# A convolution with residual: the last residual pair in one load, and a sign from VectorE ahead of the stores

## The chip, the core and the metric

The kernel runs on one core of a Trainium2 chip. The metric is the device time of one execution in microseconds; a kernel's time is the median over its executions. One execution was also recorded by the hardware profiler, and all durations and moments below are from that record, counted from the start of its span.

Five engines work side by side and meet only through semaphores: TensorE (PE) multiplies, VectorE (DVE) adds, ScalarE (ACT) converts and packs, GpSimd (POOL) clears small tiles, and SyncE (SP) issues transfers. The transfers of one issuing engine go into one queue, which 16 DMA engines share.

## What is computed

A 3 by 3 convolution with padding 1 over 16 images of 64 channels and 64 by 64 pixels, plus a residual of the output's shape, all in float32.

```python
batch, c_in, h, w, c_out, k = 16, 64, 64, 64, 64, 3
...
x_pad = np.pad(x, ((0, 0), (0, 0), (pad, pad), (pad, pad)), mode='constant')
...
output[b, co] += weight[co, ci, kh, kw] * x_pad[b, ci, kh:kh+h, kw:kw+w]
...
return (output + residual).astype(np.float32)
```

x, the residual and the output are 16.78 MB each, the weights 0.15 MB.

## The kernel before

Two images make a pair: 2 times 64 channels fill the 128 partitions, so a pair of x, of the residual or of the output is one block of 128 rows of 4096 pixels, 2 MB. There are eight pairs.

**Tiles.** `xr` holds three pairs of x as they are loaded. `xp` are four packed bf16 images: even rows of pixels in one half of the partitions, odd rows in the other. `wl` holds the rearranged weights. `ps` are two accumulators in PSUM, one image each. `ro` holds all eight pairs of the residual; the sums are written over it, and the output is stored from it.

**SyncE (lines 144 to 160 and 258 to 259)** sets the order of nearly all transfers. It loads the pairs of x, each from the fourth on when ScalarE has read the buffer it goes to (`s_half`, line 147). Behind some of them come loads of the residual, as the list `RES` says (lines 41 to 49): each entry is which pairs, which part of the pixels (`WHOLE`, `LEFT`, `RIGHT`), and the pair of x that it follows. The entry without such a number, pair 0, is issued by ScalarE at the very start. Entry i of `RES` counts on semaphore `s_r[i % 3]`, and its load waits until the entry three places before has landed (line 87). The last pair of the residual comes in two entries, 5 and 6: its left and its right half.

Then SyncE waits on line 157 until entry 5, the left half, has landed. After that it issues the early stores (`EARLY`, line 39): pairs 0 and 1, pairs 2 and 3, pairs 4 and 5, pair 6. Each waits in addition for VectorE's count of first adds, `s_add`, to show that its pairs are done, which is known from the first add of the image behind them (line 159). The last pair is stored in two halves after the block, when everything else is done (lines 258 and 259).

**ScalarE** packs each image by two copies (lines 190 and 194).

**TensorE** does for each image 24 matmuls into one accumulator (lines 238 to 255). It waits for the packed image (`s_pack`) and for an accumulator that VectorE has read (`s_bank`); the waits of lines 240 and 241 also take one off these counts. When an image is done it raises `s_conv`.

**VectorE** (lines 203 to 226) first rearranges part of the weights (line 206), then for each image adds the residual in two steps: the even rows (`par` 0), which wait for `s_conv`, and the odd rows (`par` 1). The first step raises `s_add`, the second `s_bank`. Ahead of each pair's first image it waits until the entries of `RES` that the pair needs have landed (lines 216 to 218, by the helper on line 91).

**The semaphore `s_id`** counts preparations: 12 (`NZERO`) by GpSimd's clears, one by TensorE's transposes of the weights, one each by ScalarE and VectorE when the weights are rearranged. Thus it stands at `NZERO + 3` from then on.

Of the kernel before, what the change touches and what calls it, by code (L numbers as in the profile page):

```python
# [15 lines left out]
def kernel(  # L16
# [7 lines left out]
    nc = tc.nc  # L24
# [13 lines left out]
    NZERO = 4 + 2 * NXP  # L38
    EARLY = (slice(0, 2), slice(2, 4), slice(4, 6), slice(6, 7))
    WHOLE, LEFT, RIGHT = slice(0, NPIX), slice(0, NPIX // 2), slice(NPIX // 2, NPIX)  # L40
    RES = (
        (slice(0, 1), WHOLE, None),
        (slice(1, 2), WHOLE, 1),
        (slice(2, 4), WHOLE, 3),
        (slice(4, 6), WHOLE, 5),
        (slice(6, 7), WHOLE, 7),
        (slice(7, 8), LEFT, 7),
        (slice(7, 8), RIGHT, 7),
    )
    NR = 3  # L50

    res_bc = residual.rearrange("(p b) c h w -> (b c) p (h w)", b=2)
# [18 lines left out]
    s_x = [sem(f"s_x{i}") for i in range(NXR)]  # L71
    s_r = [sem(f"s_r{i}") for i in range(NR)]
    s_out = sem("s_out")
    s_id = sem("s_id")
# [6 lines left out]
    def load_x(p):  # L81
        return nc.sync.dma_start(out=xr[p % NXR][:, :], in_=x_bc[128 * p : 128 * p + 128, :]).then_inc(s_x[p % NXR], 16)

    def load_ro(i, e):
        pairs, cols, _ = RES[i]
        if i >= NR:
            e.wait_ge(s_r[i % NR], 16 * (i // NR))
        return e.dma_start(out=ro[:, pairs, cols], in_=res_bc[:, pairs, cols]).then_inc(s_r[i % NR], 16)

    def wait_ro(e, i):  # L90
        e.wait_ge(s_r[i % NR], 16 * (i // NR + 1))

    def store(pairs, cols=slice(0, NPIX)):
        return nc.sync.dma_start(out=out_bc[:, pairs, cols], in_=ro[:, pairs, cols])
# [21 lines left out]
    def to_the_front(dma):  # L116

        def fixed(ap):  # L120
            t = ap.bass_ap.tensor.name
            return mybir.PhysicalAccessPattern(
                ap=ap.ap, offset=ap.bass_ap.offset, dtype=ap.dtype, memref=t, memsetref=t + "_set", bass_ap=ap.bass_ap
            )

        front = nc.main_func.blocks[0].instructions
        here = nc.cur_bb.bb.instructions
        ins = here.pop()
        assert ins.name == dma.ins.name
        at = next(i for i, e in enumerate(front) if e.engine == ins.engine)  # L130
        front.insert(at, copy.replace(ins, ins=[fixed(a) for a in ins.ins], outs=[fixed(a) for a in ins.outs]))
# [5 lines left out]
    def weight_block(h, half, d, par, kh):  # L137

        at = 64 * half + 32 * h
        return dict(out=wl[at : at + 32, d, :, par, :], in_=tp[0:32, kh, 0:384].rearrange("p (kw co h) -> p kw co h", kw=3, h=2)[:, :, :, h])  # L140

    with tc.tile_critical(no_gpsimd_drain=True):  # L142

        for p in range(NPAIR):
            if p >= NXR:

                nc.sync.wait_ge(s_half, 2 * (p - NXR) + 3)
            if p == 0:
                to_the_front(load_x(p))
                nc.sync.dma_start(out=wraw[:, :], in_=w_rows[:, :]).then_inc(s_w, 16)  # L150
            else:
                load_x(p)
            for i, (_, _, behind) in enumerate(RES):
                if behind == p:
                    load_ro(i, nc.sync)

        wait_ro(nc.sync, len(RES) - 2)
        for pairs in EARLY:
            nc.sync.wait_ge(s_add, 2 * pairs.stop + 1)
            store(pairs).then_inc(s_out, 16)  # L160


        nc.gpsimd.memset(ident[:, :], 0.0).then_inc(s_id, 1)  # L163
        nc.gpsimd.wait_ge(s_id, 1)
        nc.gpsimd.affine_select(  # L165
            out=ident[:, :],
            in_=ident[:, :],
            compare_op=mybir.AluOpType.not_equal,
            fill=1.0,
            base=0,  # L170
            pattern=[[-1, 128]],
            channel_multiplier=1,
        ).then_inc(s_id, 1)
        nc.gpsimd.wait_ge(s_id, 2)
        for t in xp:
            nc.gpsimd.memset(t[0:64, 0, :], 0.0).then_inc(s_id, 1)  # L176
            nc.gpsimd.memset(t[64:128, J, :], 0.0).then_inc(s_id, 1)  # L177
        nc.gpsimd.memset(wl[0:64, 0, :, 1, :], 0.0).then_inc(s_id, 1)  # L178
        nc.gpsimd.memset(wl[64:128, 1, :, 0, :], 0.0).then_inc(s_id, 1)  # L179


        to_the_front(load_ro(0, nc.scalar))
        for n in range(B):
            p, im = divmod(n, 2)
            hp = slice(64 * im, 64 * im + 64)
            x4 = xr[p % NXR].rearrange("q (j two w) -> q j two w", two=2, w=W)
            t = xp[n % NXP]
            if im == 0:
                nc.scalar.wait_ge(s_x[p % NXR], 16 * (p // NXR + 1))
            i = nc.scalar.copy(out=t[64:128, 0:J, :], in_=x4[hp, :, 0, :])  # L190
            i.then_inc(s_half, 1)
            if n >= NXP:
                i._wait_ge(s_conv, n - NXP + 1)
            nc.scalar.copy(out=t[0:64, 1 : J + 1, :], in_=x4[hp, :, 1, :]).then_inc(s_pack, 1)  # L194
            if n == 0:
                nc.scalar.wait_ge(s_id, NZERO + 1)
                for b in blocks[4:]:
                    for h in range(2):
                        i = nc.scalar.copy(**weight_block(h, *b))  # L199
                i.then_inc(s_id, 1)  # L200


        nc.vector.wait_ge(s_id, NZERO + 1)
        for k, b in enumerate(blocks[:4]):
            for h in range(2):
                i = nc.vector.tensor_copy(**weight_block(h, *b))  # L206
                if k == h == 0:
                    i.then_inc(s_bank, 2)
        i.then_inc(s_id, 1)
        for n in range(B):  # L210
            p, im = divmod(n, 2)
            hp = slice(64 * im, 64 * im + 64)
            o4 = ro[:, p, :].rearrange("q (j two w) -> q j two w", two=2, w=W)
            psj = ps[n % 2].rearrange("q c j w -> q (c j) w")
            if im == 0:
                for i, (pairs, cols, _) in enumerate(RES):
                    if pairs.start <= p < pairs.stop:
                        wait_ro(nc.vector, i)
            for par in range(2):
                i = nc.vector.tensor_tensor(  # L220
                    out=o4[hp, :, par, :], in0=psj[64 * par : 64 * par + 64, :, :], in1=o4[hp, :, par, :], op=ADD
                )
                if par == 0:
                    i._wait_ge(s_conv, n + 1)

                i.then_inc(s_add if par == 0 or n == B - 1 else s_bank, 1)


        nc.tensor.wait_ge(s_id, NZERO)
        nc.tensor.wait_ge(s_w, 16)  # L230
        wraw3 = wraw.rearrange("p (ci t) -> p ci t", t=9)
        for t in range(9):
            i = nc.tensor.transpose(  # L233
                out=tp[0:32, t // 3, 128 * (t % 3) : 128 * (t % 3) + 128], in_=wraw3[:, :, t], identity=ident[:, :]
            )
        i.then_inc(s_id, 1)
        nc.tensor.wait_ge(s_id, NZERO + 3)
        with nc.Fori(0, B // NXP, 1, engines=[PE]):
            for n in range(NXP):
                nc.tensor.wait_ge(s_bank, 1).then_inc(s_bank, -1)  # L240
                nc.tensor.wait_ge(s_pack, 1).then_inc(s_pack, -1)  # L241
                order = [(1, 0), (1, 1), (0, 0), (0, 1), (2, 0), (2, 1)]
                for i, (kw, d) in enumerate(order):
                    xlo, xhi = max(0, 1 - kw), min(W, W + 1 - kw)
                    for c in range(NCHUNK):
                        j0 = JC * c
                        m = matmul(
                            ps[n % 2][:, c, :, xlo:xhi],
                            wl[:, d, kw, :, :].rearrange("q r c -> q (r c)"),
                            xp[n][:, j0 + d : j0 + d + JC, xlo + kw - 1 : xhi + kw - 1],  # L250
                            i == 0,
                            i == len(order) - 1,
                            c == 0,
                        )
                m.then_inc(s_conv, 1)
# [37 lines left out]
```

## Time and profile before

| What | Value |
|---|---|
| median of 4 runs | 122.37 us (122.27 to 122.47) |
| the profiled execution | 122.39 us |
| its span | 120.6 us |
| mean granted TensorE clock | 0.944 |
| TensorE busy | 86.8 us (72%), 389 instructions |
| VectorE busy | 76.0 us (63%), 40 instructions |
| ScalarE busy | 63.1 us (52%), 37 instructions |
| moved by DMA | 50.48 MB, mean 419 GB/s |
| read from and written to HBM | 33.70 MB, 16.78 MB |

The span is the part of the execution that the trace covers from the first to the last of the program's own instructions; the 1.8 us between it and the execution's time lie around it. The page cuts the span into 40 slices and shows for each engine a digit, the tenths of the slice in which it was busy; the row DMA does the same for the mean of the 16 DMA engines, and the row below it gives the bytes moved per time. The chain that ended last is followed back from the last instruction of an engine; transfers that nobody on the core waits for do not stand in it. The time of a transfer is shown from its issue to its landing, that is, until its semaphore has its full count.

### The profile page before, as it was taken

What the parts mean: (1) busy time and instruction counts of PE and PEld (TensorE: products, weight loads), DVE (VectorE), ACT (ScalarE), POOL (GpSimd) and SP (SyncE); (2) the same over time, 40 slices, a digit from 0 to 9 for tenths busy, and PEclk for the clock granted to TensorE, in tenths of its full rate; (3) what the DMA queues carried; (4) which work ended last, traced back from release to release, by engine and by line L of the source; (5) the groups of instructions that cost most, each with busy time, mean ns of one, the idle gap of its engine ahead of it and who ended that gap; (6) DMA issues with size and microseconds to landing.
All of it is one profiled execution on the core that took longest, in us unless ns stands there. A gap on an engine that the chain in (4) does not pass through costs nothing.

```text
span 120.6 us, 734 instructions
## 1 busy us (share of the span) xinstructions
PE 86.8 (72%) x389; PEld 10.7 (9%) x105; DVE 76.0 (63%) x40; ACT 63.1 (52%) x37; POOL 2.4 (2%) x16
## 2 busy tenths in 40 slices
PE   0000609999999999999999999999999999100000
PEld 0000300100111111111010101010101010000000
DVE  0000180069889898798989889898898989770000
ACT  4001999999999585795956859586500000000000
POOL 5200000000000000000000000000000000000000
PEclk9999999999999999999999999999999999975555
DMA  7999999999999999999999999999999999999994
GB/s 239 408 435 429 429 435 435 435 435 413 429 435 435 435 429 424 435 435 429 424 435 429 435 435 410 432 440 435 435 429 435 429 424 429 429 435 435 413 421 177
DMA packets 3808, 50.48 MB, mean 419 GB/s; under 512 B 352, under 2 KB 480, under 8 KB 480
## 3 DMA queue, kind: packets, MB, share of 16 engines
q1 hardware_dynamic: 3664, 48.38, 94.2%
q10 hardware_dynamic: 144, 2.10, 4.1%
HBM read 33.70 MB, written 16.78 MB: 419 GB/s over the span
## 4 chain that ended last, share of the span: by engine, by line
PE 70%; DVEq 2%; DVE 2%; issue 0%
PE ps L101 53%; PE ps L100 17%; DVEq L142 2%; DVE ro L220 2%
## 5 line engine op out<-in xcount | busy, mean ns | idle before, releaser
L220 DVE TENSOR_TENSOR ro<-ps,ro 64x2048 f32<-64x2048 f32 x32 | 73.2, 2288 | 16.8 <-PE ps L101 16.3
L101 PE MATMUL ps<-xp,wl 128*128 128x504 bf16 (+1 forms) x288 | 79.3, 385 | 0.2
L190 ACT CAST xp<-xr 64x2048 bf16<-64x2048 f32 x16 | 30.3, 1896 | 21.5 <-DMA xr<-in_x_dram 11.1
L100 PE MATMUL ps<-xp,wl 128*128 128x504 bf16 (+1 forms) x92 | 35.6, 387 | 3.4 <-PEq L241 3.4
L194 ACT CAST xp<-xr 64x2048 bf16<-64x2048 f32 x16 | 30.4, 1897 | 0.4
L100 PEld LDWEIGHTS ps<-xp,wl 128*128 128x128 bf16 x96 | 9.5, 99 | 78.2 <-issue 78.2
L206 DVE CAST wl<-ps 32x192 bf16<-32x192 f32 x8 | 2.8, 348 | 14.9 <-PE ps L233 14.7
L233 PE MATMUL ps<-ident,wraw 128*32 128x128 f32 x9 | 2.1, 416 | 12.6 <-DMA wraw<-in_weight_dram 12.6
L233 PEld LDWEIGHTS ps<-ident,wraw 128*32 128x32 f32 x9 | 1.2, 140 | 13.0 <-issue 12.5
L190 ACT ACT_TABLE_LOAD x1 | 1.3, 1283 | 1.1 <-SPq L142 1.1
L199 ACT CAST wl<-ps 32x192 bf16<-32x192 f32 x4 | 1.2, 306 | 0.0
L177 POOL MEMSET xp<- 64x64 bf16 x4 | 0.6, 146 | 0.2
L176 POOL MEMSET xp<- 64x64 bf16 x4 | 0.6, 144 | 0.2
L165 POOL TENSOR_SCALAR_AFFINE_SELECT ident<-ident 128x128 f32<-128x128 f32 x1 | 0.3, 293 | 0.2 <-POOL ident L163 0.2
L179 POOL MEMSET wl<- 64x192 bf16 x1 | 0.3, 253 | 0.1
L178 POOL MEMSET wl<- 64x192 bf16 x1 | 0.3, 251 | 0.1
L163 POOL MEMSET ident<- 128x128 f32 x1 | 0.2, 205 | 0.7 <-SPq L142 0.7
L277 POOL MEMSET const-bfloat16-1.0<- 128x1 bf16 x1 | 0.1, 112 | 0.0
L277 POOL MEMSET const-uint8-127<- 128x1 uint8 x1 | 0.1, 112 | 0.0
L277 POOL MEMSET const-float32-1.0<- 128x1 f32 x1 | 0.1, 108 | 0.0
L277 POOL MEMSET const-float32-0.0<- 128x1 f32 x1 | 0.1, 103 | 0.2 <-issue 0.2
## 6 DMA issues: line engine op xcount, KB each, us to landing
xr<-in_x_dram SPq DMA_DIRECT2D x8, 2048.0 KB, 14.8
out_dram<-ro SPq DMA_DIRECT2D x3, 4096.0 KB, 20.0
ro<-in_residual_dram SPq DMA_DIRECT2D x2, 4096.0 KB, 21.1
ro<-in_residual_dram SPq DMA_DIRECT2D x2, 2048.0 KB, 18.6
ro<-in_residual_dram ACTq DMA_DIRECT2D x1, 2048.0 KB, 12.0
ro<-in_residual_dram SPq DMA_DIRECT2D x2, 1024.0 KB, 19.2
out_dram<-ro SPq DMA_DIRECT2D x1, 2048.0 KB, 14.5
out_dram<-ro SPq DMA_DIRECT2D x2, 1024.0 KB, 10.3
```

The costliest lines, as they stand in the source:

```text
L100: return e.matmul(out=out_, lhsT=lhsT, rhs=rhs, start=start, stop=stop, skip_group_check=True)
L101: return e.add_instruction(mybir.InstMatmult(name=nc.get_next_instruction_name(), engine=PE, ins=[e.lower_ap(rhs), e.lower_ap(lhsT)], outs ...
L142: with tc.tile_critical(no_gpsimd_drain=True):
L176: nc.gpsimd.memset(t[0:64, 0, :], 0.0).then_inc(s_id, 1)
L177: nc.gpsimd.memset(t[64:128, J, :], 0.0).then_inc(s_id, 1)
L190: i = nc.scalar.copy(out=t[64:128, 0:J, :], in_=x4[hp, :, 0, :])
L194: nc.scalar.copy(out=t[0:64, 1 : J + 1, :], in_=x4[hp, :, 1, :]).then_inc(s_pack, 1)
L199: i = nc.scalar.copy(**weight_block(h, *b))
L206: i = nc.vector.tensor_copy(**weight_block(h, *b))
L220: i = nc.vector.tensor_tensor(out=o4[hp, :, par, :], in0=psj[64 * par : 64 * par + 64, :, :], in1=o4[hp, :, par, :], op=ADD)
L233: i = nc.tensor.transpose(out=tp[0:32, t // 3, 128 * (t % 3) : 128 * (t % 3) + 128], in_=wraw3[:, :, t], identity=ident[:, :])
L277: nc = _bacc.Bacc("TRN2", target_bir_lowering=False, num_devices=1)
```

## The change

The two entries of the last residual pair become one, of the whole pair. The list then has six entries, and the whole load takes the place of the left half, with the same semaphore and the same wait ahead of it.

SyncE no longer waits for a landing before the early stores. It waits until `s_id` reaches `NZERO + 4`. This last count comes from VectorE: a separate increment that stands in its program behind the first add of image 10 (counted from 0, so the eleventh) and ahead of that image's second add. The waits on `s_add` ahead of each early store stay as they are, and so do the two half stores of the last pair. The wait of VectorE ahead of pair 7 covers one entry in place of two.

```diff
         (slice(6, 7), WHOLE, 7),
-        (slice(7, 8), LEFT, 7),
-        (slice(7, 8), RIGHT, 7),
+        (slice(7, 8), WHOLE, 7),
     )
+    MANY = 10
...
-        wait_ro(nc.sync, len(RES) - 2)
+        nc.sync.wait_ge(s_id, NZERO + 4)
         for pairs in EARLY:
             nc.sync.wait_ge(s_add, 2 * pairs.stop + 1)
             store(pairs).then_inc(s_out, 16)
...
                 i.then_inc(s_add if par == 0 or n == B - 1 else s_bank, 1)
+                if par == 0 and n == MANY:
+                    nc.vector.sem_inc(s_id, 1)
```

## The prediction

> **What bounds the kernel now.** I read the page's strips of busy time first, then the chain, then the waits of SyncE's queue.
>
> ```profile
> DMA  7999999999999999999999999999999999999994
> GB/s 239 408 435 429 429 435 435 435 435 413 429 435 435 435 429 424 435 435 429 424 435 429 435 435 410 432 440 435 435 429 435 429 424 429 429 435 435 413 421 177
> ...
> q1 hardware_dynamic: 3664, 48.38, 94.2%
> ...
> PE 70%; DVEq 2%; DVE 2%; issue 0%
> ```
>
> The DMA row is full from the second slice to the last but one. The chain's shares add up to 74%: it runs along TensorE from 18.0 us to 103.1 and along VectorE to 107.7, and leaves the rest to transfers. So the stream of transfers is the bound. Check: 0.69 MB move in the first 3 us (view below); the other 49.79 MB at the 431 GB/s that the stretch from 3 to 60 us shows take 115.5 us, which ends at 118.5. Measured: the last store is issued at 108.36 us and lands 11.3 us later, at 119.7; the span ends at 120.6 and the run at 122.39. Only bytes, or a hole in the stream, can move the end.
>
> ```profile
> SPq L94 <- DVE ro L220: 20.7, 2, 10.7
> SPq L94 <- DMA ro<-in_residual_dram: 16.7, 1, 16.7
> ...
> SPq L88 <- DMA ro<-in_residual_dram: 1.5, 1, 1.5
> ```
>
> These are waits of SyncE's queue (total, times, longest). The 16.7 us is the wait that the change replaces: line 157, for the left half of the last residual pair. The 1.5 us is the right half's load, held until an earlier load lands; it goes too, since the whole load takes the left half's place and its semaphore. The 20.7 us are stores waiting for VectorE, which stay.
>
> **When the stores enter the queue, and what is then left in it.**
>
> ```profile
> 58.68 2.75 SPq L88 DMA_DIRECT2D ro<-in_residual_dram  x3
> 78.17 31.40 SPq L94 DMA_DIRECT2D out_dram<-ro  x6
> ```
>
> This is SyncE's timeline: pair 6 and the two halves of pair 7 are issued from 58.68 to 61.4, the first store at 78.17. Asked one at a time, the left half issues at 59.15 and lands 19.0 us later (78.15); the right half issues at 61.10 and lands 19.5 us later (80.6). The first store therefore has 2.4 us of the right half before it. I put the end of the right half's data between 79.7 and 80.1: at the end of the span the DMA share is 0.34 from 118.6 to 119.2 us and 0.00 after, so the last store's data end at 118.8 on average and by 119.2, 0.5 to 0.9 us before its landing; 80.6 less that is 79.7 to 80.1.
>
> ```profile
> 75.00:78.00 3.00, 3.00 (x15) 0.37 (x4) 2.42 (x2) 1.63 (x2) 0.00 (x0) 1.00 1.00 421
> 78.00:81.00 3.00, 3.00 (x15) 0.29 (x3) 2.97 (x2) 2.93 (x2) 0.00 (x0) 1.00 1.05 448
> 81.00:84.00 3.00, 3.00 (x15) 0.39 (x4) 2.42 (x2) 1.68 (x1) 0.00 (x0) 1.00 0.99 426
> ```
>
> The last two columns of these stretches are the DMA share and GB/s. Loads give way to stores at full share: there is no hole here that an earlier issue could close, so moving the stores forward gains nothing.
>
> **How late a store may be issued** follows from the start, where the queue is empty.
>
> ```profile
> DMA  0000000000000999907595700099559955909999
> ...
> DMA packets 42, 0.69 MB, mean 229 GB/s; under 512 B 0, under 2 KB 0, under 8 KB 0
> ```
>
> This is the stretch 0 to 3 us in 40 slices of 0.075 us. The first load is issued at 0.00; the first packet comes in the fourteenth slice, at 0.98 us. On average over the engines it is later: 0.69 MB at 431 GB/s is 1.60 us of work, so 1.40 us passed empty. A store costs nothing if it is issued 1.4 us before the loads' data end, at 78.3 to 78.7. The old issue, 78.17, is just inside.
>
> The Trainium skill ("DMA: Bandwidth & Descriptors", section "Anatomy of one DMA — SWDGE (gpsimd) path") would make such a margin matter little: it holds the fixed cost of a DMA to be mostly completion latency, not setup. By that rule even an issue at 79.4 would leave 122.4. The 0.98 to 1.40 us of the empty start, issued by SyncE, disagree, and they decide.
>
> **When VectorE gives the sign.** The added increment stands behind the eleventh image's first add and ahead of its second.
>
> ```profile
> 77.13 4.61 DVE L220 TENSOR_TENSOR ro<-ps,ro 64x2048 f32<-64x2048 f32 x2 [0.58 <-PE ps L101]
> ```
>
> That add starts at 77.13 and lasts 2.28 us, to 79.42. An increment that stands alone on VectorE does not occur in this trace, so I bound it: at the add's start (77.15) or at its end (79.43). Two rows speak for the start. The first pair shows semaphore waits of VectorE itself:
>
> ```profile
> L91 DVEq EVENT_SEMAPHORE  x1: 21/21/21, 15.9 to 15.9; - x1
> ```
> ```profile
> L206 DVE CAST wl<-ps x8: 345/348/351, 14.7 to 17.3; 32x192 bf16<-32x192 f32 x8
> ```
>
> The wait of line 91 stands behind all eight casts, the last of which starts at 17.3, and is done at 15.9: VectorE's queue handles a lone semaphore instruction while earlier work is still to run. The second is on TensorE's queue, and it does change a semaphore:
>
> ```profile
> L241 PEldq EVENT_SEMAPHORE  x1: 51/51/51, 30.1 to 30.1; - x1
> ```
>
> Line 241 takes one off s_pack for the third image at 30.1, and the second image's last matmul, in front of it, ends only when VectorE's add for it starts, at 30.45. So a lone semaphore instruction is not held until the work ahead of it has finished. I take 77.15. Evidence for the other end is the DRAIN of line 142 on VectorE, 4.64 us from 103.1, which does stay until both last adds are done; but that is a drain, and the diff asks for an increment. SyncE follows at once: the third store is issued at 89.82, when the thirteenth image's first add (start 87.51, 2.28 us) ends at 89.79. Hence the first store at about 77.2, 1.0 us earlier than before and 1.1 to 1.5 us ahead of the point where lateness begins to cost.
>
> **The sum, part by part.**
> - One 2 MB load for two of 1 MB. Pair 7 of x lands at 70.9, residual pair 6 (2 MB whole) at 75.8, the halves at 78.15 and 80.6: 4.9 us whole, 4.8 in halves. At the end the whole 2 MB store takes 4.9 (109.8 to 114.7), two halves 5.0 (114.7 to 119.7). The halves thus cost between 0.1 less and 0.1 more than a whole; I take a gain of 0.03 us.
> - One DMA issue fewer on SyncE (0.33 us) and the 1.5 us wait before it: both lay under SyncE's wait for the left half, so 0. Without that cover there is still the queue: at 59.15 it holds 19 us of loads, so an issue some us earlier or later starts no byte sooner.
> - The wait on s_id: behind it on SyncE stand only the three waits of the early stores and those stores; nobody but GpSimd's final wait needs them. At 77.2 the loads are still running. 0.
> - The increment on VectorE: between 0.02 us (the 21 ns of line 91) and the remainder of an add, were it to hold the queue. VectorE idles 0.58 us before each image, which covers 0.02. Were it not covered, VectorE's and TensorE's later images would be late; but the next store of VectorE's work is issued at 89.82 with the stream full to 100.1 (second store, 78.6 plus 21.4), and the last pair at 107.96 with it full to 114.7. That lane may be some 5 us late (114.7 less 107.96 less 1.4) before the end moves.
> - VectorE's waits for pair 7 fall from two to one, in one instruction of 49 ns at 92.7, under the add; pair 7 lands 12 us before. 0.
>
> Sum: 122.39 - 0.03 = 122.36 on the profiled execution, whose time is 0.02 above the median of the four runs (122.27 to 122.47). I predict 122.35.
>
> The same section of that page of the Trainium skill gives a fit, for transfers issued by GpSimd, of about 2.0 us fixed per DMA on top of its bytes; one DMA fewer would by it give 120.4, an estimate. The landings (4.9 us whole, 4.8 in halves) show no such cost inside a full queue.
>
> **The rivals.**
> 1. The sign comes when the add is finished, 79.43 (slower). One mechanism: the queue runs empty between loads and stores. The first packet follows 0.98 to 1.40 us after the issue, at 80.4 to 80.85; the data of the loads end at 79.7 to 80.1; the hole is 0.3 to 1.15 us, most likely 0.9 (the mean delay of 1.40 after the mid end, 79.9): 122.7 to 123.5, centre 123.25. It decides from an issue later than about 78.5. For it: the DRAIN row, and that all of VectorE's other increments ride on finished work. Against it: lines 91 and 241. Chance 0.22.
> 2. The sign slips to the end of the second add, 81.74: a hole of 81.75 + 1.4 - 79.9 = 3.3 us, 125.7. Against it: that add already carries an increment of its own, of another semaphore, and the new one stands ahead of it. Chance 0.03.
> 3. A whole transfer runs better than two halves by more than the landings show, or a transition costs something: faster than 122.13. The shares of 1.00 and 1.05 speak against it. With the scatter between draws of runs, chance 0.10.
> 4. The change doesn't do what it says: the sign goes up earlier, as soon as VectorE's queue has it, near the tenth image's first add (71.95). Then the stores queue behind loads earlier and the stream stays full: no change, 122.35. This counts with the forecast.
>
> **The numbers.** The forecast and rival 4 have 0.65, with 122.15 to 122.55 as their own range (scatter of the four runs, 0.1 either way, with the 0.1 of the landings). Holding eight in ten needs rival 1, so the range reaches to 123.4. A measurement here tells about 0.2% (0.24 us) from no change. Faster 0.10; same 0.63, the forecast less 0.02 for scatter; slower 0.27, rivals 1 and 2 with that scatter.
>
> **What would show it.** Right: the first store issued near 77.2, SyncE's wait of some 15.7 us put down to VectorE, the DMA strip full from 78 to 82, landings 80.6 and about 90.3. A first store at 79.4 with a DMA share under 0.8 between 79.5 and 81, and every later landing late by the same amount, is rival 1. A last landing before 119.4 with the strip as full as now would show rival 3. The forecast falls with any hole in the strip, wherever it is.

## The result, and the profile after

| | before | changed |
|---|---|---|
| median | 122.35 us (60 runs, 122.19 to 122.49) | 122.48 us (40 runs, 122.32 to 122.73) |
| ratio | | 1.0010, 95% interval 1.0006 to 1.0015 |
| the profiled execution | 122.39 us | 122.50 us |
| its span | 120.56 us | 120.57 us |
| its time less its span | 1.83 us | 1.93 us |

The changed kernel is 0.1% slower, and clearly so: the whole interval of the ratio lies above 1. The forecast was 122.35, no change, in a range up to 123.4 that was left open for a late store. The last two rows of the table show where to look: the two spans are equal to 0.01 us, so the difference is not among the transfers that the prediction was about.

The page of the changed kernel, transfers and chain:

```profile
DMA  7999999999999999999999999999999999999993
GB/s 239 429 429 412 431 435 429 435 435 435 435 429 429 424 435 424 424 424 435 435 429 429 435 435 435 435 435 435 424 429 435 429 429 435 435 435 429 402 429 163
...
q1 hardware_dynamic: 3520, 48.38, 94.2%
...
PE 71%; DVEq 2%; DVE 2%; issue 0%
```

The stream is as full as before, with 144 packets fewer for the same bytes: the whole load has 128 rows of 16 KB where the halves had 256 of 8 KB, and 16 completion packets fewer. SyncE's waits in the changed kernel (total, times, longest):

```profile
SPq L94 <- DVE ro L220: 21.7, 2, 11.7
SPq L94 <- DVEq L228: 17.5, 1, 17.5
```

Line 228 is the sign. When it comes, and what it releases, is in three answers: the sign itself, VectorE's timeline around it, and SyncE's timeline.

```profile
L228 DVEq EVENT_SEMAPHORE  x1: 21/21/21, 77.7 to 77.7; - x1
```
```profile
77.67 4.61 DVE L220 TENSOR_TENSOR ro<-ps,ro 64x2048 f32<-64x2048 f32 x2 [0.58 <-PE ps L101]
```
```profile
59.21 0.91 SPq L88 DMA_DIRECT2D ro<-in_residual_dram  x2
77.73 32.38 SPq L94 DMA_DIRECT2D out_dram<-ro  x6
```

The increment is done at 77.7, when the eleventh image's first add has just started (77.67) and not when it ends (79.96); the first store follows at 77.73. VectorE adds with the same 0.58 us of idle time in front. Now the handover from loads to stores, stretch by stretch, with the DMA share and GB/s last:

```profile
77.00:79.00 2.00, 2.00 (x11) 0.21 (x3) 1.42 (x2) 1.33 (x1) 0.00 (x0) 1.00 0.99 426
79.00:81.00 2.00, 2.00 (x11) 0.27 (x3) 1.97 (x2) 1.98 (x2) 0.00 (x0) 1.00 0.98 418
81.00:83.00 2.00, 2.00 (x11) 0.19 (x2) 1.42 (x2) 0.63 (x2) 0.00 (x0) 1.00 1.09 467
```

There is no hole. Inside the span the handover went as the forecast had it.

### The profile page after: what moved, and what is told of

Same layout as the page of the kernel before. It is cut to its first block, busy times and chain, and to the rows that moved or that the text cites. A ratio compares the mean times of both kernels' runs of the same rounds, so it can differ in the third digit from the quotient of the medians.

```text
span 120.6 us, 734 instructions
## 1 busy us (share of the span) xinstructions
PE 87.2 (72%) x389; PEld 10.6 (9%) x105; DVE 76.0 (63%) x40; ACT 63.1 (52%) x37; POOL 2.4 (2%) x16
## 4 chain that ended last, share of the span: by engine, by line
PE 71%; DVEq 2%; DVE 2%; issue 0%
PE ps L101 53%; PE ps L100 17%; DVEq L142 2%; DVE ro L220 2%
```

## The experiments

Two questions: which part of the change makes the 0.13 us, and what would the sign have cost had it come at another time. "Rest" below is the time of an execution less its span, as a mean over the executions of that kernel. It is a sharper measure than the time, since the span scatters by some 0.1 us from one execution to the next and the rest by 0.03 (the spans of the timed executions are on record to 0.1 us, which is most of these 0.03; one kernel, with two increments, scatters more).

### The kernel before against itself

> The kernel before, unchanged, timed against itself: how small a difference counts, and how time divides into span and what lies outside it. Every theory: ratio 1.000 within 0.0005, 122.35 us. The profiled execution's time less its span: 1.83 us as in the profile of before (1.93 in the profile of the changed kernel). If it scatters between 1.83 and 1.93 here, the theory that the added time lies outside the span falls.

Measured: 122.35 us, ratio 0.9996 (0.9987 to 1.0005), rest 1.82 in 11 executions. Over the four groups of comparison runs the kernel before shows a mean span of 120.56 and a rest of 1.83 in 101 executions. The changed kernel shows 120.55 and 1.93 in 42. So of its 0.13 us some 0.10 are rest. The other 0.03 stand in neither the spans nor the rests; the two medians come from different sets of executions.

### The sign alone, heard by nobody

```diff
                 i.then_inc(s_add if par == 0 or n == B - 1 else s_bank, 1)
+                if par == 0 and n == MANY:
+                    nc.vector.sem_inc(s_id, 1)
```

added to the kernel before, which keeps its halves and its wait for the left half.

> The kernel before with nothing but VectorE's increment added; SyncE still waits for the landing of the left half, nobody hears the sign. Theory A (the changed kernel's 0.13 us lie outside the span, at the end of the program, and come with the one more instruction on VectorE): 122.45 to 122.50 us, time less span 1.93. Theory B (they come with the transfers: the whole load or the earlier stores): 122.35, time less span 1.83. Theory C (they come with the one transfer fewer on SyncE's program): 122.35.

Measured: 122.56 us, ratio 1.0016 (1.0007 to 1.0025), rest 1.96. The increment is enough: theory A. Theories B and C have neither their load nor their issue changed here, and the time is there all the same. It lies above the expected 122.45 to 122.50, because the mean span of these 11 executions is 120.63, 0.06 above that of the kernel before and within its scatter.

### The sign without the whole load

The changed kernel with `LEFT` and `RIGHT` back in the list.

> The changed kernel with the last residual pair loaded in halves as before: the sign alone is left of the change. First store at 77.2 to 77.7 us, DMA full around it under all theories. Theory A: 0.04 us above the changed kernel (the halves cost that in the transfers' own records), 122.50 to 122.55 us. Theory B with the whole load at fault: 122.35. Theory B with the earlier stores at fault: 122.48. Theory C: 122.35.

Measured: 122.45 us, ratio 1.0009 (1.0000 to 1.0018), rest 1.95. The rest stays with the sign, as theory A says, though the time is below the 122.50 to 122.55 expected. Whether the halves cost 0.04 us on top can't be told from 11 executions (mean span 120.55).

### The whole load without the sign

The kernel before with the whole entry in the list. Its line 157, `wait_ro(nc.sync, len(RES) - 2)`, now means the landing of pair 6, so that the stores are issued earlier, at 75.9.

> The whole load alone, no sign: SyncE waits for the landing of the residual's pair 6 (entry 4 of 6) ahead of the stores, so the first store is issued near 75.8 us, some 4.8 us of loads still in front of it. Theory A: 122.31 us (0.04 saved by the whole load, nothing added outside the span, time less span 1.83). Theory B with the whole load at fault: 122.48. Theory C (one transfer fewer on SyncE lengthens the end): 122.45, time less span 1.93.

Measured: 122.91 us, ratio 1.0044 (1.0029 to 1.0059). The rest is 1.83, so theory C falls. But the mean span is 121.12, half a microsecond longer, which no theory had said. SyncE's timeline and the handover:

```profile
58.60 0.91 SPq L87 DMA_DIRECT2D ro<-in_residual_dram  x2
75.87 32.95 SPq L93 DMA_DIRECT2D out_dram<-ro  x6
```
```profile
77.00:79.00 2.00, 2.00 (x11) 0.20 (x2) 1.95 (x1) 1.92 (x2) 0.00 (x0) 1.00 1.27 451
79.00:81.00 2.00, 2.00 (x11) 0.24 (x3) 1.97 (x2) 1.87 (x1) 0.00 (x0) 1.00 0.72 279
81.00:83.00 2.00, 2.00 (x11) 0.25 (x3) 1.42 (x2) 0.76 (x1) 0.00 (x0) 1.00 1.03 442
```

With the stores issued at 75.87, the stretch from 79 to 81 moves 279 GB/s in place of 418. (A packet counts in the stretch in which it starts, hence the share over 1 before.) In the trace's packets the queues are not empty: load packets of 16 KB, which take 611 ns around them, take up to 1213 ns here; 32 take over 640, from 77.8 us on. What they take beyond 611 adds up to 0.58 us for each of the 16 engines, and the load is complete 0.63 us later than the 4.863 us that it takes in the changed kernel would have it (mean over the engines). So the loss is nearly all in these packets: an early store slows the load in front of it.

### The sign from TensorE, at no instruction

```diff
-        nc.sync.wait_ge(s_id, NZERO + 4)
+        nc.sync.wait_ge(s_conv, MANY + 1)
...
-                if par == 0 and n == MANY:
-                    nc.vector.sem_inc(s_id, 1)
```

in the changed kernel: TensorE's count goes up when the eleventh image is multiplied, which is what the sign's add waits for.

> The changed kernel without the increment on VectorE: SyncE waits for TensorE's count of finished images, s_conv at 11 or more, which goes up at the moment at which the eleventh image's first add starts. So the stores are issued at the same time as in the changed kernel (77.2 to 77.7 us), with no instruction added. Theory A (the added 0.1 us come from the increment on VectorE, at the end of the program): time less span back at 1.83, 122.31 to 122.37 us, ratio 0.9995 to 1.000. If the earlier stores or the whole load are at fault: 122.45 to 122.5.

Measured: 122.42 us, ratio 1.0003 (0.9994 to 1.0011), rest 1.82. The rest is back with the increment gone. The time lies above the expected 122.31 to 122.37, by the span: it is 120.64 on average and 120.90 in the profiled execution; there TensorE was early, the first store was issued at 76.73, and the handover shows a smaller form of the loss of the run before:

```profile
77.00:79.00 2.00, 2.00 (x11) 0.28 (x3) 2.00 (x1) 1.98 (x2) 0.00 (x0) 1.00 1.10 426
79.00:81.00 2.00, 2.00 (x11) 0.21 (x3) 1.97 (x2) 1.56 (x1) 0.00 (x0) 1.00 0.88 377
```

Eleven of the load's packets take over 640 ns here (up to 1153), against 32 with the store at 75.87 and none at 77.42 (a later run) and 77.73. Their excess is 0.21 us for each engine, and the load is complete 0.21 us late.

### The late sign

The same kernel, with `s_add` in place of `s_conv`: SyncE waits for the end of the eleventh image's first add.

> The late sign of rival 1: SyncE waits until the eleventh image's first add is finished (s_add at 11 or more), the whole load as in the changed kernel, no increment on VectorE. First store at 79.5 to 80.0 us. By the prediction's working the queue runs empty for 0.3 to 1.15 us: 122.7 to 123.5, most likely 123.2, with a DMA share clearly under 1 between 79.5 and 81.5 and all later landings late by the same. If an empty queue costs nothing: 122.35.

Measured: 122.76 us, ratio 1.0047 (1.0018 to 1.0075), mean span 121.14; the 12 executions run from 122.34 to 123.98. The median falls into a gap: six of them took 122.34 to 122.57, six 122.96 to 123.98. The profiled one, at 122.98, is of the second six; SyncE's timeline and the handover:

```profile
79.61 30.18 SPq L94 DMA_DIRECT2D out_dram<-ro  x6
```
```profile
78.00:79.50 1.50, 1.50 (x9) 0.12 (x2) 1.50 (x1) 1.48 (x2) 0.00 (x0) 1.00 1.07 459
79.50:80.00 0.50, 0.50 (x4) 0.07 (x1) 0.47 (x2) 0.50 (x1) 0.00 (x0) 1.00 0.24 98
80.00:80.50 0.50, 0.50 (x4) 0.10 (x1) 0.50 (x1) 0.50 (x1) 0.00 (x0) 1.00 0.01 0
80.50:81.00 0.50, 0.50 (x5) 0.00 (x0) 0.50 (x1) 0.50 (x1) 0.00 (x0) 1.00 1.22 524
```

This is rival 1's hole. The store is issued at 79.61, the loads' data end at 79.9 on average, and the stores' first packets start at 80.53 to 80.68 on the 16 engines: 0.92 to 1.07 us after the issue. From this issue the prediction's delay of 1.40 would make a hole of 1.1 us; the delay is about 1.0, and the hole some 0.65 us. The delay was read from the empty start, where the first packets are slow as well: they start 1.01 to 1.67 us after the issue and take 674 to 1462 ns in place of 611.

What parts the two sixes stands beside their times: the mean granted clock is 0.940 to 0.941 in the six that lost little or nothing and 0.943 to 0.948 in the others. In the profiles of this study an execution with a mean clock of 0.940 or 0.941 has the end of the eleventh image's first add at 78.97 to 79.34 us, and one with 0.944 to 0.948 at 79.32 to 79.95 (why, see below). So, as an estimate from these rows, a sign that comes at about 79.3 or before is still in time. The dearest executions lost up to 1.6 us, more than a delay of 1.0 explains; no profile of them was kept.

### More increments, and one on another engine

```diff
+                if par == 0 and n in (8, 9, 10):
+                    nc.vector.sem_inc(s_id, 1)
```

in the kernel before:

> The kernel before with three unheard increments on VectorE, behind the first adds of images 8, 9 and 10. If each costs at the end of the program: time less span 1.83 + 3 x 0.11 = 2.16, 122.7 us. If the cost comes once, with a length that the program passes: 1.93 to 1.95, 122.45 to 122.55. If it is taken up where the increment stands: a longer span in place of a longer rest.

Measured: 122.64 us, ratio 1.0023 (1.0014 to 1.0032), mean span 120.55, rest 2.12. More increments, more rest, none of it in the span. The trace of this kernel has something that the changed kernel's has not, one transfer after the span's end (stretch from 121.5 to 124 us of each; the first fence is three increments, the second the changed kernel):

```profile
DMA packets 1, 0.01 MB, mean 3 GB/s; under 512 B 0, under 2 KB 0, under 8 KB 0
...
q14 instruction: 1, 0.01, 1.2%
```
```profile
DMA packets 0, 0.00 MB, mean 0 GB/s; under 512 B 0, under 2 KB 0, under 8 KB 0
```

It is a fetch of instructions, 8192 bytes at 122.24 us, 1.80 us after the span's end.

On ScalarE, `nc.scalar.sem_inc(s_id, 1)` behind the second copy of image 10:

> The kernel before with one unheard increment on ScalarE, behind the second copy of image 10. If any added instruction lengthens the end: time less span 1.93, 122.45 us or more. If VectorE's program alone is the one that is waited for at the end: 1.83, 122.35 us.

Measured: 122.34 us, ratio 1.0000 (0.9991 to 1.0009), rest 1.82. So an added instruction does not cost on every engine: on ScalarE it is free.

### The length of VectorE's program

If every instruction of VectorE costs 0.1 us, taking some out should gain. Ahead of pairs 3 and 5 it waits for residual entries that it has already waited for with pairs 2 and 4:

```diff
-                    if pairs.start <= p < pairs.stop:
+                    if pairs.start == p:
```

> The kernel before without two waits of VectorE that an earlier wait already covers (ahead of pairs 3 and 5, whose residual came with pairs 2 and 4): VectorE's program is two instructions shorter. If every instruction of VectorE's program costs 0.1 us at the end: time less span 1.63, 122.15 to 122.2 us. If the cost comes only past the length that the kernel before has: 1.83, 122.35 to 122.4.

> The changed kernel without the same two waits: VectorE's program is one instruction shorter than in the kernel before, with the sign in it. If the length of VectorE's program is what counts, under either form: time less span 1.83 or less, 122.3 to 122.4 us. If it is the increment itself, whatever the length: 1.93, 122.45 to 122.5.

Measured: the kernel before with two waits fewer, 122.70 us, ratio 1.0026 (1.0015 to 1.0037), rest 2.22. The changed kernel with two fewer, 122.85 us, ratio 1.0034 (1.0021 to 1.0047), rest 2.23. Neither theory: taking instructions out costs more than putting them in, and again outside the span (120.54 and 120.60). So it is not a price per instruction. What is left to try is the length itself. The condition `and p != 3`, added to the line as it was, takes out a single wait:

> The changed kernel without one covered wait of VectorE (ahead of pair 3): the sign is in it, and VectorE's program has as many instructions as in the kernel before. If the length alone decides: time less span 1.83, 122.3 to 122.4 us. If the increment itself costs 0.1 us at the end: 1.93, 122.48 us. If a missing wait costs, as in the run with two fewer: 2.2, 122.75 us.

> The kernel before without that one wait: VectorE's program one instruction shorter. By the length (the changed kernel with two fewer waits has this length and showed 2.23): time less span 2.2, 122.75 us. If a wait more or less matters by itself, half of what two showed: 2.03, 122.55 us. If only the second wait matters: 1.83, 122.35 us.

> The kernel before with two unheard increments on VectorE: one instruction longer than the changed kernel. One showed 1.94 to 1.95 us of time less span, three showed 2.11. If each adds alike: 2.03, 122.55 us. If the cost comes in steps: 1.95 or 2.11.

Measured: the changed kernel with one wait fewer, 122.38 us, ratio 1.0000 (0.9991 to 1.0009), rest 1.82. The kernel before with one fewer, 122.73 us, ratio 1.0034 (1.0023 to 1.0044), rest 2.24. The kernel before with two increments, 122.58 us, ratio 1.0016 (1.0007 to 1.0025), rest 2.04; here the rest scatters from 1.79 to 2.18 between executions, so that the mean doesn't tell an even price from steps.

The waits are counted in the profile on line 91: the kernel before, one fewer, two fewer.

```profile
L91 DVEq EVENT_SEMAPHORE  x8: 21/21/49, 15.9 to 92.7; - x8
```
```profile
L91 DVEq EVENT_SEMAPHORE  x7: 21/21/50, 15.8 to 92.6; - x7
```
```profile
L91 DVEq EVENT_SEMAPHORE  x6: 21/21/50, 15.9 to 92.5; - x6
```

All kernels, by the number of VectorE's instructions in the trace (the 40 of the page are only those that keep the engine busy; here waits, increments and drains count too):

| VectorE's instructions | kernels | rest, us |
|---|---|---|
| 55 | two waits fewer | 2.22 |
| 56 | one wait fewer; changed with two waits fewer | 2.24; 2.23 |
| 57 | before; changed with one wait fewer; sign from TensorE; increment on ScalarE; the late sign and the three with a store at 75.7 to 75.9 | 1.83; 1.82; 1.82; 1.82; 1.81 to 1.84 |
| 58 | changed; increment alone; sign with halves | 1.93; 1.96; 1.95 |
| 59 | two increments | 2.04 (1.79 to 2.18) |
| 60 | three increments | 2.12 |

Kernels of one length agree within 0.03 us, whatever their instructions are; lengths differ by up to 0.4. The length of the kernel before is the best of the six, and no kernel of this study was measurably faster than it. Every edit that changed the length put in or took out a lone semaphore instruction, a wait or an increment. So the runs do not tell the length of the program from the number of such instructions in it.

Where in the rest it lies, the trace's semaphore records show in part. After the span one semaphore is raised twice in nine steps; the first nine come at the same times in all kernels, within 0.04 us. These are the times of the second nine, in us after the span's end:

```
instructions, kernel       4th step  6th step  9th step
57 before                      1.70      1.83      1.95
58 changed                     1.81      1.93      2.05
58 increment alone             1.80      1.93      2.04
56 one wait fewer              1.71      2.23      2.35
57 changed, one wait fewer     1.71      1.83      1.95
55 two waits fewer             1.71      1.83      1.95
```

At 58 the fourth step is late by 0.1, at 56 the sixth by 0.4, as much as the rest is longer. At 55 none is, and nothing in the trace shows where its 0.4 us lie. At 59 and 60 a fetch of instructions starts 1.86 and 1.80 us after the span, before the ninth step. Which engine makes which step, and why a length is late, stays open.

### What makes an early store cost

> The whole load with the first store at the landing of pair 6 (near 75.8 us) as in the run that lost 0.6 us there, but the second store held until TensorE's count stands at 11 (76.7 to 78.2). If the loss came from both stores queued behind five and more packets of a load: no loss or a part, 122.3 to 122.6 us, and pair 7's packets at their 0.611 us. If the first store's early issue alone makes it: 122.9 us again.

> The kernel before with the same early stores, at the landing of pair 6 (near 75.8 us), and the last residual pair in halves. If the loss comes with early stores whatever the load's form: 122.9 us, span 121.1. If it needs the whole load: 122.35 to 122.4, span 120.56.

The first is the whole load with the first store at the landing of pair 6 and `nc.sync.wait_ge(s_conv, 11)` ahead of the second; the second is the kernel before with `len(RES) - 3` on line 157. Measured: 122.91 us, ratio 1.0036 (1.0023 to 1.0049), stores at 75.89 and 78.44, mean span 121.06; and 122.98 us, ratio 1.0046 (1.0033 to 1.0058), first store at 75.74, mean span 121.18. So neither the second store nor the form of the load makes it: one store issued early is enough. The stretch from 79 to 81 us of each moves less than the 418 GB/s of the changed kernel, first the one with the second store held, then the one with halves:

```profile
79.00:81.00 2.00, 2.00 (x12) 0.20 (x2) 1.97 (x2) 1.98 (x2) 0.00 (x0) 1.00 0.88 352
```
```profile
79.00:81.00 2.00, 2.00 (x11) 0.29 (x3) 1.97 (x2) 1.68 (x1) 0.00 (x0) 1.00 1.02 377
```

Why the DMA engines take longer for a load's packets then stays open.

## Why the prediction was wrong, point by point

**The step that failed** is the fourth of the sum: "The increment on VectorE: between 0.02 us (the 21 ns of line 91) and the remainder of an add, were it to hold the queue. VectorE idles 0.58 us before each image, which covers 0.02." It looked for the cost where the instruction stands, and there it was right: 21 ns, covered. The cost is 0.10 us at the program's end: rest 1.83 to 1.93. The sum began with the old execution's time, and so took over the 1.8 us around the span as a constant. The increment alone shows it (1.96), the same sign with the old length of the program removes it (1.82, 122.38 us). What makes the rest depend on VectorE's program stays open.

**Right in mechanism.**
- What bounds the kernel: the stream of transfers. The changed kernel's is as full, and its span equal.
- The sign comes at the add's start: 77.7 and 77.67 us. Rivals 1 and 2 are not this kernel.
- No hole at the handover. The store at 77.73 came half a microsecond later than the predicted 77.2 because TensorE's lane was later in this execution, and still in time. That it was not too early either is luck: the prediction saw no cost on that side (see rival 4).
- The whole load's gain, put at 0.03 us: by the completion packets in the trace, the mean over the engines, the last residual pair takes 4.906 us in halves and 4.863 whole, and the last store's data end 0.046 us earlier. The last landing, which the slowest engine sets, is at 119.66 in both profiles.

**Right in kind, wrong in size.** Rival 1 as a kernel of its own: its queue does run empty, but its median of 122.76 us lies inside the range of 122.7 to 123.5 only as the middle of two groups, 122.34 to 122.57 and 122.96 to 123.98. The mis-sized term is the delay from issue to first packet, taken as 1.40 us from the empty start; it measured 0.92 to 1.07. What was missing is that the moment of the add itself moves, from free to late.

**Wrong.**
- Rival 4 had an earlier sign at no cost ("the stores queue behind loads earlier and the stream stays full"). A first store at 75.7 to 75.9 costs 0.5 to 0.6 us of span, and one at 76.73 still 0.3 in its profiled execution; none was tried at rival 4's own 71.95. The time for the first store is bounded on both sides: by these profiles it loses at 76.73 and not at 77.42, and not at 78.2 but at 79.61.
- The prediction took the moment of the eleventh image from one profile. In the seventeen profiles of this study that image's first add starts anywhere from 76.69 to 78.39 us. The traces show what moves it: TensorE's matmuls take 0.43 us each until the record of full granted clock begins and 0.22 after it, and that beginning lies between 20.83 and 24.17 us. The earliest goes with the add at 76.69, the latest with the one at 78.39; in the kernel before it is 21.75. The landing of the left half, the old sign, puts the first store between 78.12 and 78.26 in eight profiles. The change thus trades a sign that keeps time with the transfers for one that does not. Its own executions hint at a price: the three with a mean clock of 0.939 to 0.941, where the add is early, took 122.53, 122.68 and 122.73, against the median of 122.48. Three are too few to show it.

## What to carry to other kernels

Look at both parts: the span, and the time less the span. An instruction that costs nothing where it stands may cost 0.1 us at the end of the program. Where a few tenths of a per cent matter, the same edit should be tried at the same program length before its cost is put down to what it does. Where a store is to follow loads without a gap, tie its issue to a landing in the same queue and not to a computation, and try both an earlier and a later point: here each had its price.

## What the runs showed of the hardware that was not expected

- The time outside the span goes with the length of VectorE's program (or the number of its lone semaphore instructions), up and down: 2.22, 2.24, 1.83, 1.93 to 1.96, 2.04 and 2.12 us at 55 to 60 instructions. One more on ScalarE changed nothing.
- The Trainium skill ("Runtime: NRT & Kernel Launch", section "Instruction fetch mechanics") says that an engine fetches its instructions in 16 KiB blocks by DMA while it runs, and that crossing a block is mostly hidden. The traces with 59 and 60 instructions show one fetch of 8192 bytes behind the span, and mean rests of 2.04 and 2.12 against 1.83 in the kernel before. At 55, 56 and 58 no such fetch is recorded and the rest is long too, so the page's rule alone doesn't explain the table.
- A store issued 4 us before the data of the loads in front of it end makes those loads' 16 KB packets take up to 1213 ns in place of 611; issued 2.5 us before (at 77.42), it does not.
- From a store's issue to its first packet, on a queue that runs empty 0.3 us after the issue: 0.92 to 1.07 us in the run with the late sign.
